# Block inverse of the gated delta rule: its 32- and 64-wide levels as tile products of the new blocks alone, the other triangle by transposing

## The chip, the cores and the metric

The kernel runs on one core of a Trainium2 chip, as one program with one launch. The metric is the time of an execution on the device in microseconds (us). In the profile PE is the tensor engine's matrix products, PEld its weight loads, DVE the vector engine, ACT the scalar engine, POOL the general engine, SP the engine that issues most transfers.

## The reference, cut to what matters

The program is two transformer blocks on 256 tokens of width 1024. The change lies in the first block's second layer, a gated delta rule with eight heads, 128 channels a head and, in the reference, chunks of 64 tokens:

```python
decay = jnp.exp(jnp.where(causal, g[..., :, None] - g[..., None, :], -jnp.inf))
a = jnp.einsum('bhncd,bhnmd->bhncm', k_beta, k) * decay
m = jnp.where(strict, a, 0.0) + jnp.eye(CHUNK, dtype=jnp.float32)
rhs = jnp.concatenate([v * beta[..., None], k_beta * jnp.exp(g)[..., None]], axis=-1)
sol = lax.linalg.triangular_solve(m, rhs, left_side=True, lower=True, unit_diagonal=True)
...
def step(state, xs):
    u_c, w_c, qk_c, qd_c, kd_c, gl_c = xs
    v_new = u_c - jnp.einsum('bhcd,bhde->bhce', w_c, state)
    o_c = (jnp.einsum('bhcd,bhde->bhce', qd_c, state)
           + jnp.einsum('bhcm,bhme->bhce', qk_c, v_new))
    state = state * gl_c[..., None, None] + jnp.einsum('bhcd,bhce->bhde', kd_c, v_new)
    return state, o_c
```

So in each head and chunk a unit lower triangular system is solved. The kernel takes chunks of 128 tokens, two halves of the 256, and inverts the 128x128 triangular matrix of each head and half.

## The kernel before

The program runs in phases (a pooling layer, an MLP, the delta rule, an MLP, an attention and gating mixer, a gated MLP, a last layer). Engines run their own queues in order; a scheduler fills these queues from the order in which the program is written, moves work that is ready ahead, and is held by `after("pe")` (L274), which lets an instruction be issued only behind the last matrix product recorded in `ends["pe"]`. No order is written by hand beyond the list `steps` in `gdn` (L508).

The matrices of four heads go together: a *chain* is a half h and a group g of four heads, four chains in all. Each has a tile `Ls` (128 tokens, 4 heads, 128 tokens; the negated strictly triangular part, tile name L), `Ts` (the inverse so far, lower triangle, tile name bc, one tile for both halves of a group) and `Rs` (its transposed, upper triangle, tile name Rm). `solve_base` (L630) inverts the 16x16 diagonal blocks on the vector engine and makes `Rs` by a transposition.

Then the inverse is built up in three levels (`LEVELS`, L25: 16, 32, 64): two neighbouring blocks of that width are joined to one of twice the width. `level_up` (L690) forms Y = L'R over the whole 128x128 matrix, four heads, and multiplies it with a mask `ups[li]` that keeps only the corner blocks that are new at this level (rows of the even block, columns of the odd one). `level_down` (L695) forms R·Y and adds it to R; unless the level is the last, it also forms the transposed product and adds it to T. `products` (L658) issues four products, one a head, into one PSUM bank; each is an fp32 product of 128x128 by 128x128. Banks come from three pools: psa (four buffers), psm and psc (two each).

`steps` (L757) runs first `sides` (transposed keys and values, key-query products) for the four chains, then the levels in a skewed order: at step t the down of the item two back, then the up of item t; the items are level 0 of the four chains, level 1 of the four, level 2 of the four. So a chain's up and down are two steps apart, and a chain comes back with its next level after four. Behind them stand `solution` (L702, R times the right-hand side), the new state, the output, and the output projection, whose weights (in_gdn_w_out) are cast on ACT (L141) and subtracted on DVE (L142) while the levels run.

Of the kernel before, what the change touches and what calls it, by code (L numbers as in the profile page):

```python
# [13 lines left out]
ALU = mybir.AluOpType  # L14
AX = mybir.AxisListType
P = 128
# [7 lines left out]
BASE = 16  # L24
LEVELS = (16, 32, 64)  # L25


def shape_constants():

    i = np.arange(P)  # L30
    a, b = i[:, None], i[None, :]
    f = np.float32
    ident = (a == b).astype(f)
    cum = np.concatenate([(a <= b).astype(f), np.ones((P, P), f)], 1)
    causal = np.concatenate([np.zeros((P, P), f), np.where(b <= a, f(0), f(NEG))], 1)
    block = (a // BASE == b // BASE).astype(f)
    ups = [((a // (2 * s) == b // (2 * s)) & ((a // s) % 2 == 0) & ((b // s) % 2 == 1)).astype(f) for s in LEVELS]
    sel = np.zeros((P, 16), f)
    for r in range(0, P, 32):
        sel[r : r + 16] = -np.eye(16)  # L40
    tri = np.concatenate([ident, cum, causal, block] + ups, 1)
    pos = np.arange(T)
    near, far = [], []
    for w in WINDOWS:
        m = ((pos[:, None] <= pos[None, :]) & (pos[None, :] - pos[:, None] < w)) / np.minimum(pos + 1, w)[None, :]
        m = (m - np.eye(T)).astype(f)
        near.append(m[:P, :EDGE])
        far.append(m[P:, P:])
    return np.ascontiguousarray(tri), np.ascontiguousarray(np.concatenate(near + far, 1)), sel
# [3 lines left out]
def tile_two_blocks(ctx: ExitStack, tc: tile.TileContext, I, tri_d, band_d, sel_d, out):  # L53
    nc = tc.nc
    pe, act, dve, pool, sp = nc.tensor, nc.scalar, nc.vector, nc.gpsimd, nc.sync
# [18 lines left out]
    def work(shape, tag, bufs, dt=F32):  # L74

        return ph[0].tile(shape, dt, tag=tag, bufs=bufs, name=f"{tag}_{next(ids)}")
# [12 lines left out]
    def bank(k):  # L89
        return banks[k].tile([P, 512], F32, tag=k, name=f"ps{k}_{next(ids)}")  # L90

    def quads(k):
        return bank(k).rearrange("p (a t) -> p a t", t=P)
# [6 lines left out]
    ident = cp.tile([P, P], F32, name="ident")  # L100
    tri = cp.tile([P, tri_d.shape[1] - P], F32, name="tri")
    cumf = tri[:, 0 : 2 * P]
    cumu, ones = cumf[:, :P], cumf[:, P:]
    causal = tri[:, 2 * P : 4 * P]
    block = tri[:, 4 * P : 5 * P]
    ups = [tri[:, (5 + i) * P : (6 + i) * P] for i in range(len(LEVELS))]
    mhalf = cp.tile([P, 16], F32, name="mhalf")
    pool.memset(mhalf, -0.5)

# [161 lines left out]
    ends = {}  # L271
# [230 lines left out]
    def bc4(m):  # L502
        return m.unsqueeze(1).to_broadcast([P, 4, P])
# [4 lines left out]
    def gdn(xs, X, then):  # L508
# [37 lines left out]
        for h in range(2):  # L546
            ps = bank("c")
            pe.matmul(ps[:, 0:8], cumu, gg[:, h, :], start=True, stop=True)
            pe.matmul(ps[:, 8:16], ones, gg[:, h, :], start=True, stop=True)
            a, b, c = (cp.tile([P, 8], F32, name=f"{n}{h}") for n in ("gc", "eg", "ed"))  # L550
# [38 lines left out]
        Ls, Ts, Rs = {}, {}, {}  # L589
# [68 lines left out]
        def products(bk, lhs, rhs):  # L658

            ps = quads(bk)  # L660
            for a in range(4):
                ends["pe"] = pe.matmul(ps[:, a, :], lhs[:, a, :], rhs[:, a, :], start=True, stop=True).ins
            return ps
# [23 lines left out]

        rhs, kd, state, Ym, xv, ob = {}, {}, {}, {}, {}, {}

        def level_up(c, li):  # L690
            yp = products("a", Ls[c], Rs[c])
            Ym[c] = work([P, 4, P], "Ym", 2)
            dve.tensor_tensor(Ym[c], yp, bc4(ups[li]), ALU.mult)

        def level_down(c, li):  # L695
            rp = products("m", Ts[c], Ym[c])
            if li < len(LEVELS) - 1:
                tp = products("c", Ym[c], Ts[c])
                dve.tensor_tensor(Ts[c], tp, Ts[c], ALU.add)
            dve.tensor_tensor(Rs[c], rp, Rs[c], ALU.add)  # L700

        def solution(h, g):  # L702
            xp = products("a", Rs[h, g], rhs[h, g])
# [53 lines left out]
        steps = [(sides, c) for c in chains]  # L757
        up_down = [(c, li) for li in range(len(LEVELS)) for c in chains]
        for t in range(len(up_down) + 2):
            if t > 1:  # L760
                steps.append((level_down, up_down[t - 2]))
            if t < len(up_down):
                steps.append((level_up, up_down[t]))
        pair = lambda f, *a: [(f, (*a, g)) for g in range(2)]
        steps += pair(solution, 0)
        for g in range(2):
# [331 lines left out]
    with phase("gdn"):  # L1098
        xs, X, emb = gdn(xs, X, lambda: layer_normed(lgs[1, 0], lbs[1, 0]))
# [38 lines left out]
```

## Time and profile before

| what | us |
|---|---|
| median of 3 runs (range) | 1129.73 (1128.65 to 1130.77) |
| the profiled execution | 1129.11 |
| its span in the profile | 1127.4 |
| first up product of level 0 | at 359.36 |
| first product of `solution` | at 388.93 |

A profile's group line reads: source line, engine, operation, tiles written and read, shape, count; then the time in which at least one of them ran, the mean duration of one in ns, and the idle time of the engine ahead of them with what ended it. A matrix product in fp32 leaves two records in the trace, a transposition one. Their durations overlap, since products are pipelined, so the price of one is the distance between starts. "L662" is the product line of the helper `products`, which serves many places; tile names tell them apart. Engine idle time matters only on the engine that sets the length of a stretch.

### The profile page before, as it was taken

To read this page: it belongs to the slowest core of one execution; us is meant where nothing else is said; L and a number is where in the kernel's file an instruction comes from. 1 tells how busy PE (TensorE), PEld (TensorE's weight loads), DVE (VectorE), ACT (ScalarE), POOL (GpSimd) and SP (SyncE) were. 2 spreads that over 40 slices of the span, in tenths; PEclk is the share of its full clock that TensorE was granted. 3 is DMA by queue.
4 is the path that set the end of the run, shared out by engine and by line. 5 is a ranking of instruction groups with operands and counts; after the bars stand their busy time and mean duration, and the time that the engine had idled before them with its cause. 6 is when DMAs were issued, how large, how long until landed. Compare 5 with 4: busy or idle time off the path is not lost. (4 is left out here: it accounts for less than half of the span.)

```text
span 1127.4 us, 17109 instructions
## 1 busy us (share of the span) xinstructions
PE 1098.7 (97%) x6546; PEld 964.2 (86%) x6546; DVE 798.4 (71%) x1265; ACT 603.4 (54%) x982; POOL 79.6 (7%) x78
## 2 busy tenths in 40 slices
PE   7999999999999999999999999999999999999997
PEld 5688888899999988788888788898888799999986
DVE  5865555688898668755557775587786867677784
ACT  1754544556656155554546456566664655555663
POOL 1001111110201010011101200000000000000000
PEclk9999999999999999999999999999999999999999
DMA  9665656545446035865666656565435745666650
GB/s 338 226 214 186 195 181 200 182 139 171 115 121 185 20 112 187 262 195 184 198 185 212 206 166 186 141 198 170 132 113 168 216 149 185 188 190 180 188 203 38
DMA packets 145250, 197.92 MB, mean 176 GB/s; under 512 B 11136, under 2 KB 117648, under 8 KB 145168
## 3 DMA queue, kind: packets, MB, share of 16 engines
q1 hardware_dynamic: 145167, 196.83, 56.6%
q8 instruction: 51, 0.84, 0.3%
q14 instruction: 32, 0.25, 0.1%
HBM read 195.49 MB, written 1.31 MB: 175 GB/s over the span
## 5 line engine op out<-in xcount | busy, mean ns | idle before, releaser
L142 DVE TENSOR_TENSOR lo<-raw,hi 128x1024 fp32r<-128x1024 f32 (+4 forms) x322 | 383.1, 1199 | 176.7 <-ACT hi L141 172.4
L141 ACT CAST hi<-raw 128x1024 fp32r<-128x1024 f32 (+4 forms) x322 | 330.8, 1031 | 175.4 <-PE psm L243 54.8
L243 PE MATMUL psm<-X,hi 128*128 128x512 f32 x864 | 308.3, 400 | 2.6 <-DVE sum L246 2.6
L244 PE MATMUL psm<-X,lo 128*128 128x256 f32 x864 | 242.2, 280 | 0.0
L243 PEld LDWEIGHTS psm<-X,hi 128*128 128x128 f32 x864 | 162.2, 188 | 44.7 <-DVE sum L246 4.7
L244 PEld LDWEIGHTS psm<-X,lo 128*128 128x128 f32 x864 | 163.1, 189 | 1.1
L153 PE MATMUL psm<-X,lo 128*128 128x256 f32 x448 | 127.1, 284 | 0.5 <-DVE lo L142 0.5
L152 PE MATMUL psm<-X,hi 128*128 128x256 f32 x448 | 126.9, 283 | 0.0
L151 PE MATMUL psm<-X,hi 128*128 128x256 f32 x448 | 126.9, 284 | 0.0
L151 PE MATMUL psa<-hi,hh 128*128 128x512 f32 x296 | 115.6, 391 | 0.0
L152 PE MATMUL psa<-lo,hh 128*128 128x512 f32 x296 | 115.5, 390 | 0.0
L153 PE MATMUL psa<-hi,hl 128*128 128x512 f32 x296 | 115.2, 389 | 0.0
L153 PEld LDWEIGHTS psm<-X,lo 128*128 128x128 f32 x448 | 85.9, 192 | 0.7 <-DVE lo L142 0.7
L151 PEld LDWEIGHTS psm<-X,hi 128*128 128x128 f32 x448 | 85.8, 192 | 0.6 <-ACT X L193 0.2
L152 PEld LDWEIGHTS psm<-X,hi 128*128 128x128 f32 x448 | 86.0, 192 | 0.3
L245 ACT COPY sum<-psm 128x256 f32<-128x256 f32 x120 | 44.1, 367 | 63.0 <-PE psm L244 62.8
L152 PE MATMUL psa<-lo,X 128*128 128x512 f32 (+5 forms) x212 | 76.0, 359 | 1.7 <-DVE lo L142 1.7
L151 PE MATMUL psa<-hi,X 128*128 128x512 f32 (+5 forms) x212 | 76.2, 360 | 0.5 <-ACT hi L141 0.5
L246 DVE TENSOR_TENSOR sum<-psm,sum 128x256 f32<-128x256 f32 x120 | 50.4, 420 | 37.1 <-ACT sum L245 37.1
L153 PE MATMUL psa<-hi,X 128*128 128x512 f32 (+5 forms) x212 | 75.9, 358 | 0.0
L451 POOL TENSOR_TENSOR hl<-sum,hh 128x512 fp32r<-128x512 f32 x32 | 43.4, 1355 | 330.8 <-ACT hh L450 164.8
L153 PEld LDWEIGHTS psa<-hi,hl 128*128 128x128 f32 x296 | 55.6, 188 | 11.9
(340 smaller groups left out, 1723.1 us busy)
## 6 DMA issues: line engine op xcount, KB each, us to landing
raw<-in_mlp_w_dram SPq DMA_DIRECT2D x128, 512.0 KB, 4.1
raw<-in_w_in_dram SPq DMA_DIRECT2D x48, 512.0 KB, 4.7
raw<-in_w_up_dram SPq DMA_DIRECT2D x44, 512.0 KB, 4.1
raw<-in_gdn_w_in_dram SPq DMA_DIRECT2D x24, 512.0 KB, 4.5
raw<-in_w_down_dram SPq DMA_DIRECT2D x22, 512.0 KB, 4.5
raw<-in_ple_gate_w_dram SPq DMA_DIRECT2D x16, 512.0 KB, 6.0
raw<-in_gdn_w_out_dram SPq DMA_DIRECT2D x8, 512.0 KB, 5.0
raw<-in_w_branch_a_dram SPq DMA_DIRECT2D x8, 512.0 KB, 4.9
```

The source lines that it names most:

```text
L141: act.copy(hi, raw)
L142: dve.tensor_tensor(lo, raw, hi.bitcast(F32), ALU.subtract)
L151: pe.matmul(o, lh, rh, start=start, stop=False)
L152: pe.matmul(o, lh, rl, start=False, stop=False)
L153: ends["pe"] = pe.matmul(o, ll, rh, start=False, stop=stop).ins
L243: pe.matmul(ps, wh, X.parts(k), start=k == 0, stop=False)
L244: ends["pe"] = pe.matmul(ps[:, 1, :], wl, X.hi(k), start=False, stop=k == 7).ins
L245: act.copy(y[:, f, :], ps[:, 0, :])
L246: dve.tensor_tensor(y[:, f, :], ps[:, 1, :], y[:, f, :], ALU.add)
L451: pool.tensor_tensor(hl, r, hh.bitcast(F32), ALU.subtract)
```

## The change

Level 0 keeps its full-width products with the mask. At levels 1 and 2 `level_up` and `level_down` now compute the corner blocks alone: for each head and each corner one product of 32x32 (two corners a head, so eight products a group) or 64x64 (one corner a head, four products). The results are copied out without mask or addition, since a corner is empty before: Y by DVE, R by ACT. The transposed product and its addition are gone at every level; `level_turn` transposes R instead and copies the result to T on ACT, four steps behind the up: whole 128x128 matrices after level 0, the upper left 64x64 after level 1, none after level 2. Only the mask of level 0 is left, so the constant tensor `tri` is 256 columns narrower.

```diff
-    ups = [tri[:, (5 + i) * P : (6 + i) * P] for i in range(len(LEVELS))]
+    ups = tri[:, 5 * P : 6 * P]
...
+        def corners(li):
+
+            n = LEVELS[li]
+            return [(slice(i, i + n), slice(i + n, i + 2 * n)) for i in range(0, P, 2 * n)]
+
         def level_up(c, li):
-            yp = products("a", Ls[c], Rs[c])
             Ym[c] = work([P, 4, P], "Ym", 2)
-            dve.tensor_tensor(Ym[c], yp, bc4(ups[li]), ALU.mult)
+            if li == 0:
+                dve.tensor_tensor(Ym[c], products("a", Ls[c], Rs[c]), bc4(ups), ALU.mult)
+                return
+            ps = quads("a")
+            for a in range(4):
+                for ev, od in corners(li):
+                    ends["pe"] = pe.matmul(ps[ev, a, od], Ls[c][od, a, ev], Rs[c][od, a, od], start=True, stop=True).ins
+            for ev, od in corners(li):
+                dve.tensor_copy(Ym[c][ev, :, od], ps[ev, :, od])
 
         def level_down(c, li):
-            rp = products("m", Ts[c], Ym[c])
-            if li < len(LEVELS) - 1:
-                tp = products("c", Ym[c], Ts[c])
-                dve.tensor_tensor(Ts[c], tp, Ts[c], ALU.add)
-            dve.tensor_tensor(Rs[c], rp, Rs[c], ALU.add)
+            if li == 0:
+                dve.tensor_tensor(Rs[c], products("m", Ts[c], Ym[c]), Rs[c], ALU.add)
+                return
+            ps = quads("m")
+            for a in range(4):
+                for ev, od in corners(li):
+                    ends["pe"] = pe.matmul(ps[ev, a, od], Ts[c][ev, a, ev], Ym[c][ev, a, od], start=True, stop=True).ins
+            for ev, od in corners(li):
+                act.copy(Rs[c][ev, :, od], ps[ev, :, od])
+
+        def level_turn(c, li):
+
+            ps, n = quads("c"), P if li == 0 else P // 2
+            for a in range(4):
+                ends["pe"] = pe.transpose(ps[:n, a, :n], Rs[c][:n, a, :n], ident[:n, :n]).ins
+            act.copy(Ts[c][:n, :, :n], ps[:n, :, :n])
...
             if t < len(up_down):
                 steps.append((level_up, up_down[t]))
+            if 4 <= t < len(up_down):
+                steps.append((level_turn, up_down[t - 4]))
```

In the changed file the up products of levels 1 and 2 stand on line L704, their copies on L706, the down products on L715, their copies on L717, the transpositions on L723, their copies on L724; the masks are L699 and the additions to R L710.

The first place is PE from the first chain's up of level 1 on. Before, full groups stood there in a row (psa is an up, psm a down for R, psc a down for T; behind the arrow the moving tile and the weights):

```order
L662 MATMUL psa_3581<-Rm_2698,L_2401 128x128 x4
L662 MATMUL psm_3588<-Ym_3567,bc_2617 128x128 x4
L662 MATMUL psc_3593<-bc_2617,Ym_3567 128x128 x4
L662 MATMUL psa_3600<-Rm_2718,L_2607 128x128 x4
L662 MATMUL psm_3607<-Ym_3586,bc_2411 128x128 x4
```

Now the same place holds, up to the end of the 32-wide items:

```order
L704 MATMUL psa_3564<-Rm_2698,L_2401 32x32 x8
L723 MATMUL psc_3575<-ident,Rm_2698 128x128 x4
L662 MATMUL psm_3581<-Ym_3550,bc_2617 128x128 x4
L704 MATMUL psa_3588<-Rm_2718,L_2607 32x32 x8
L723 MATMUL psc_3599<-ident,Rm_2718 128x128 x4
L715 MATMUL psm_3605<-Ym_3563,bc_2411 32x32 x8
L704 MATMUL psa_3617<-Rm_2708,L_2433 32x32 x8
L723 MATMUL psc_3628<-ident,Rm_2708 128x128 x4
L715 MATMUL psm_3634<-Ym_3587,bc_2617 32x32 x8
L704 MATMUL psa_3646<-Rm_2728,L_2639 32x32 x8
L723 MATMUL psc_3657<-ident,Rm_2728 128x128 x4
L715 MATMUL psm_3663<-Ym_3616,bc_2411 32x32 x8
```

The third group of each step is a transposition in place of the product for T, and tiles of 32 and of 128 take turns. Level 2 follows directly on PE:

```order
L704 MATMUL psa_3675<-Rm_2698,L_2401 64x64 x4
L723 MATMUL psc_3681<-ident,Rm_2698 64x64 x4
L715 MATMUL psm_3687<-Ym_3645,bc_2617 32x32 x8
L704 MATMUL psa_3699<-Rm_2718,L_2607 64x64 x4
L723 MATMUL psc_3705<-ident,Rm_2718 64x64 x4
L715 MATMUL psm_3711<-Ym_3674,bc_2411 64x64 x4
L704 MATMUL psa_3718<-Rm_2708,L_2433 64x64 x4
L723 MATMUL psc_3724<-ident,Rm_2708 64x64 x4
```

From there to the solutions all groups are 64 wide but the one of 32. The second place is DVE around the weight subtraction L142 that lies among the levels. Before:

```order
L693 TENSOR_TENSOR Ym_3548<-psa_3543,tri 128x512
L142 TENSOR_TENSOR qkv_3965<-raw_3963,qkv_3964 128x1024
L699 TENSOR_TENSOR bc_2617<-psc_3555,bc_2617 128x512
L700 TENSOR_TENSOR Rm_2718<-psm_3550,Rm_2718 128x512
L693 TENSOR_TENSOR Ym_3567<-psa_3562,tri 128x512
```

Now (Ym_3550 is the mask of the fourth chain at level 0, which psm_3581 above reads):

```order
L699 TENSOR_TENSOR Ym_3537<-psa_3538,tri 128x512
L710 TENSOR_TENSOR Rm_2718<-psm_3544,Rm_2718 128x512
L142 TENSOR_TENSOR qkv_4005<-raw_4003,qkv_4004 128x1024
L699 TENSOR_TENSOR Ym_3550<-psa_3551,tri 128x512
L710 TENSOR_TENSOR Rm_2708<-psm_3557,Rm_2708 128x512
L706 COPY Ym_3563<-psa_3564 32x4x32 x2
```

The subtraction stands directly ahead of the fourth mask; the additions to T are gone, and from level 1 on each step has two small copies. The third place is ACT, which had nothing between the weight cast and the solutions' copies:

```order
L141 CAST qkv_3964<-raw_3963 128x1024
L705 COPY Ym_3726<-psa_3721 128x512
L705 COPY Ym_3733<-psa_3728 128x512
L710 COPY L_3740<-psm_3735 128x512
L732 ACTIVATE sq_3747,co_2385<-psa_3742 128x128 x3
```

Now the copies to T and R stand between them:

```order
L141 CAST qkv_4004<-raw_4003 128x1024
L724 COPY bc_2411<-psc_3575 128x512
L724 COPY bc_2617<-psc_3599 128x512
L717 COPY Rm_2698<-psm_3605 32x4x32 x2
L724 COPY bc_2411<-psc_3628 128x512
L717 COPY Rm_2718<-psm_3634 32x4x32 x2
L724 COPY bc_2617<-psc_3657 128x512
```

They come behind the cast, which waits for a transfer of weights.

More of the change, by code (lines that the diff above doesn't have):

```diff
@@ L36, in shape_constants @@
     block = (a // BASE == b // BASE).astype(f)
-    ups = [((a // (2 * s) == b // (2 * s)) & ((a // s) % 2 == 0) & ((b // s) % 2 == 1)).astype(f) for s in LEVELS]
+    ups = ((a // (2 * BASE) == b // (2 * BASE)) & ((a // BASE) % 2 == 0) & ((b // BASE) % 2 == 1)).astype(f)
     sel = np.zeros((P, 16), f)
@@ L40, in shape_constants @@
         sel[r : r + 16] = -np.eye(16)
-    tri = np.concatenate([ident, cum, causal, block] + ups, 1)
+    tri = np.concatenate([ident, cum, causal, block, ups], 1)
     pos = np.arange(T)
```

## The prediction

> **What bounds the kernel now.** I read the page's busy shares first, then the granted clock and busy time of the block inverse and of what follows it, then that stretch's groups and its timeline.
>
> ```profile
> PE 1098.7 (97%) x6546; PEld 964.2 (86%) x6546; DVE 798.4 (71%) x1265; ACT 603.4 (54%) x982; POOL 79.6 (7%) x78
> ```
>
> TensorE (PE) is busy 97% of the span, so a microsecond taken from PE inside the inverse should reach the end, if the inverse itself is bound by PE. The windows answer that; behind the busy times stand the granted clock, the DMA share and GB/s.
>
> ```profile
> 359.36:361.90 2.54, 1.95 (x18) 1.79 (x17) 2.54 (x6) 1.47 (x8) 0.00 (x0) 1.00 0.00 0
> 361.90:388.93 27.03, 27.03 (x240) 26.95 (x241) 21.27 (x31) 1.05 (x1) 0.00 (x0) 1.00 0.13 40
> 388.93:414.93 26.00, 25.16 (x172) 22.63 (x170) 14.04 (x39) 17.79 (x56) 4.03 (x4) 1.00 0.23 81
> ```
>
> The three levels run from 359.36 to 388.93, 29.57 us. After one wait at the start PE never stops (27.03 of 27.03); VectorE (DVE) has 5.8 us spare, ScalarE (ACT) works 1.05 us, the DMA queues rest, the clock is full. PE alone sets the length. In its groups (busy, mean ns, idle before):
>
> ```profile
> L662 PE MATMUL psm<-Ym,bc 128*128 128x128 f32 x96 | 12.7, 277 | 0.6 <-DVE Ym L693 0.6
> L662 PE MATMUL psa<-Rm,L 128*128 128x128 f32 x96 | 12.5, 275 | 0.0
> L662 PE MATMUL psc<-bc,Ym 128*128 128x128 f32 x64 | 8.5, 275 | 0.0
> L693 DVE TENSOR_TENSOR Ym<-psa,tri 128x512 f32<-128x512 f32 x12 | 8.2, 689 | 1.8 <-PE psa L662 1.8
> L700 DVE TENSOR_TENSOR Rm<-psm,Rm 128x512 f32<-128x512 f32 x12 | 8.3, 690 | 2.7 <-PE psm L662 2.7
> L699 DVE TENSOR_TENSOR bc<-psc,bc 128x512 f32<-128x512 f32 x8 | 5.5, 690 | 1.2 <-PE psc L662 1.2
> ```
>
> An fp32 product of four heads leaves eight records; 96+96+64 records are 32 such groups. The busy times are unions with overlap, so the price is taken from starts:
>
> ```profile
> 361.07 1.28 DVE L693 TENSOR_TENSOR Ym<-psa,tri 128x512 f32<-128x512 f32 x2
> 361.90 1.13 PE L662 MATMUL psm<-Ym,bc 128*128 128x128 f32 x8 [0.59 <-DVE Ym L693]
> ...
> 377.16 1.06 PE L662 MATMUL psa<-Rm,L 128*128 128x128 f32 x8
> 378.06 1.06 PE L662 MATMUL psm<-Ym,bc 128*128 128x128 f32 x8
> 378.25 0.69 DVE L693 TENSOR_TENSOR Ym<-psa,tri 128x512 f32<-128x512 f32 x1 [0.20 <-PE psa L662]
> ```
>
> Group to group is 0.894 us (377.16 to 378.06), 0.112 a record. DVE starts 0.03 behind the last record's end (377.16 + 1.06 = 378.22). Two groups from 359.36 fill PE to 361.15; the third starts at 361.90, since VectorE comes late to the first mask (361.07; two in 1.28, so the first ends near 361.75): a wait of 0.65 beyond the usual step. 32 x 0.894 = 28.6, this wait and 0.3 at the end make the 29.57.
>
> **The change, step by step.** Level 0 (16 wide) keeps four up and four down groups: 8 x 0.894 = 7.15, and the wait of 0.65. Its four transposed products go; four transpositions come, of four records each:
>
> ```profile
> 356.05 0.60 PE L668 MATMUL psc<-ident,qkv 128*128 128x128 f32 x4
> 356.49 0.83 PE L662 MATMUL psa<-qkv,qkv 128*128 128x128 f32 x6
> ```
>
> 0.44 a group, 1.75 in all. Levels 1 and 2 had 20 full groups, 17.9 us. Now level 1 has eight groups of eight 32x32 products (16 records if fp32 still leaves two) and four of 64x64 transpositions; level 2 has eight groups of four 64x64 products. No row shows such a tile. Bounds come from how a record scales with the moving width:
>
> ```profile
> L372 PE MATMUL psa<-pw,pl 128*128 128x256 f32 x32 | 7.1, 379 | 0.0
> 264.05 0.37 PE L549 MATMUL psc<-gg,tri 128*128 128x8 f32 x2
> 264.27 0.37 PE L548 MATMUL psc<-gg,tri 128*128 128x8 f32 x2
> 791.31 1.14 PE L926 MATMUL psa<-bc,m 128*64 128x128 f32 x12
> ```
>
> At 256 columns a record is 7.1/32 = 0.222, twice the 0.112 at 128: no fixed part shows. So 64 wide is 0.056 and 32 wide 0.028, half of that (0.014) if a group's two corners, which lie in different rows and columns of the array, run at once. The other end is the product with eight moving columns and full weights: two records in 0.22, still 0.11. The nearest row is L926, weights 64 wide in two halves of the array: (1.14 - 0.28)/11 = 0.078 a record, 1.4 times the 0.055 of two perfect halves, at twice to four times our widths. I take 0.035 for a 32-wide record (0.028 and a quarter more), corners one after the other, and 0.056 for a 64-wide one. Level 1: 8 x 16 x 0.035 = 4.5; level 2: 8 x 8 x 0.056 = 3.6; the small transpositions 16 x 0.055 = 0.9.
>
> Changing the tile has a price in the trace, where 128-row products meet a 44-row transposition and where they meet L926:
>
> ```profile
> 911.39 0.28 PE L152 MATMUL psm<-X,hi 128*128 128x256 f32 x1
> 911.51 0.28 PE L153 MATMUL psm<-X,lo 128*128 128x256 f32 x1
> 911.72 0.25 PE L123 MATMUL psc<-ident,rows 44*128 44x44 f32 x1
> 911.90 0.39 PE L151 MATMUL psm<-X,hi 128*128 128x256 f32 x1
> 791.10 0.28 PE L244 MATMUL psm<-X,lo 128*128 128x256 f32 x1
> ```
>
> The usual step behind such a record is 0.12 (911.39 to 911.51). Here it is 0.21 into the small tile, and into L926 likewise 0.21 (791.10 to 791.31): 0.09 per change of tile. The new order has 13 changes (128 to 32 and back for each turn, then 32 to 64): 1.2 us. The Trainium skill ("TensorEngine Tiling (Array Packing)", Key Properties) says that changing the tiling mode drains TensorE; the trace agrees, with 0.09 us. Without a drain the sum would be 1.2 shorter. The same page (Gotcha 1: PSUM Pressure) says that different row tiles cannot access one PSUM bank at once; both corners of a group write one bank, and no run here shows such a pair. By it the corners go one after the other, 0.56 a group; without it 0.28, 2.2 us less in all.
>
> Waits. New hops run over ACT, and the copies are small:
>
> ```profile
> 909.10 0.27 ACT L124 COPY taps<-psc 128x128 f32<-128x128 f32 x1 [0.48 <-PE psc L123]
> 264.45 0.17 DVE L551 COPY gc<-psc 128x8 f32<-128x8 f32 x1 [0.24 <-PE psc L549]
> 390.02 0.59 ACT L705 COPY Ym<-psa 128x512 f32<-128x512 f32 x1 [24.21 <-PE psa L662]
> 364.77 1.05 ACT L141 CAST qkv<-raw 128x1024 fp32r<-128x1024 f32 x1 [3.64 <-DMA raw<-in_gdn_w_out_dram]
> 365.85 1.23 DVE L142 TENSOR_TENSOR qkv<-raw,qkv 128x1024 fp32r<-128x1024 f32 x1 [0.30 <-ACT qkv L141]
> ```
>
> A 32x4x32 copy is 128 elements a row: 0.27 on ACT; on DVE, between 0.17 at eight elements and 0.69 at 512, about 0.3. In a level-1 turn of the order PE has 0.56 down, 0.56 up, 0.44 transposition and two changes, 1.74 us; ACT has 2 x 0.27 + 0.59 = 1.13, DVE 0.6, and each result has a turn or more before its reader. ACT and DVE hide there; if a 32-row copy cost as much as a full one (0.59), ACT's 1.77 would just match PE. Two waits do show. The weight cast at 364.77 stands ahead of ACT's first turn copy; it ends at 365.82 and by the sum PE ends that turn's transpositions after 367, so this costs nothing (were the transfer late, every turn copy would queue behind it). On DVE its subtraction (365.85 to 367.08) stands ahead of the mask of the fourth chain: that mask ends near 367.7, and the fourth down group, due near 367.5 by the sum, waits 0.3. At the end the last down group waits 0.2 for its copy, since no other group is left to cover it.
>
> The sum: 7.15 + 0.65 + 1.75 + 4.5 + 3.6 + 0.9 + 1.2 + 0.5 + 0.1 = 20.35 us against 29.57: 9.2 less. DVE's 13 us fewer count nothing, being hidden already. The mask tensor's transfer shrinks by a quarter, which is hidden:
>
> ```profile
> L1095 SPq DMA_DIRECT2D tri<-in_tri_dram x1: 327/327/327, 14.7 to 14.7; - x1
> ...
> DMA to landing us min/median/max: 7.3/7.3/7.3
> ```
>
> It lands near 22 us, and the first reader shown above (L549 at 264.05) comes 240 us later. No other transfer changes its place in SP's queue, and POOL's order stays. Behind the inverse PE is busy 25.16 of 26.00 with DMA at 0.23, and weights for the next stage are fetched when their buffers come free, which moves with PE: I let the gain through. The profiled execution took 1129.11 us (span 1127.4); 9.2 less is 1119.9. The median shown, 1129.73, is 0.62 higher, so the forecast for a median is **1120.5**.
>
> **Rivals.** *Corners overlap*: a 32-wide group costs 0.28, ACT's 1.13 still fits into the 1.18 of a turn, and 11.4 us go: 1118.3. For it: in L926 the two halves do run together. Against: those share their rows. *Small records have a floor of some 0.06, or waits of 0.3 in ten turns*: all but the small records is 10.85 us (7.15 + 0.65 + 1.75 + 1.2 + 0.1), and 208 of them (128 + 64 + 16) at 0.062 make 12.9, together 23.75, 5.8 less: 1123.9. L926's 0.078 speaks for it, L372 against. The Trainium skill ("TensorE: Matmul & The Clock Gate", "Wait — 56ns, not 53.3ns?") gives 62 ns of sequencer time per MATMUL with hardware decode off and a 25 ns floor otherwise; the rows are too wide to decide. *A flat record price, slower than before*: a record costs 0.11 whatever its width, as L549's does. 208 x 0.111 + 10.85 = 33.9, 4.4 more: 1134.1. It turns slower from 0.090 a record on, (29.57 - 10.85)/208. L926's 0.078 is below that and L549 has full-width weights, so I hold it unlikely. *The gain is lost behind the inverse*: PE would have to wait 9 us there for weights; it is idle 0.84 of those 26.00 now. No change, 1129.
>
> **How the numbers follow.** Forecast (8 to 10.5 us less) 0.52; overlap 0.15; floor or waits (3 to 8 less) 0.20; flat price 0.08; lost 0.05. The range goes from the overlap's far end, 1117.5, to 1125.5, which is a record of 0.07; what lies beyond is the flat price, the lost gain and the dear end of the floor. 0.2% is 2.3 us, about what a measurement can tell here. Faster 0.87, no change 0.05, slower 0.08.
>
> **What would show it.** The solutions (two groups reading Rm with rhs) should start near 380 instead of 388.93; L704 and L715 starts give the record price directly; the step between a 32-wide group and a full transposition shows the change of tile; PE's idle time ahead of L662 and L715 shows the waits. The prediction is wrong if a 32-wide group takes over 0.9 us, if PE waits for ACT copies in every turn, or if the stretch from 389 to 460 grows by what the inverse loses.

## The result and the profile after

| | before | after |
|---|---|---|
| median of 4 runs (range), us | 1129.19 (1127.41 to 1130.77) | 1119.45 (1118.92 to 1121.0) |
| the profiled execution, us | 1129.11 | 1119.24 |
| its span, us | 1127.4 | 1117.5 |
| first up product to first `solution` product, us | 29.57 | 19.03 |
| from there to the end of the span, us | 738.46 | 737.86 |

The ratio of the medians is 0.9916, with a 95% interval of 0.9898 to 0.9935: the change saves 9.7 us. Forecast were 9.2, and 1120.5 us. The three levels are now 10.54 us shorter, and what follows them is as long as it was to within 0.6 us; this execution came to the levels 1.3 us later than that of before (360.64 against 359.36), which hides a part of it in the span.

The busy times on the page of the changed kernel:

```profile
PE 1088.5 (97%) x6578; PEld 952.1 (85%) x6578; DVE 785.9 (70%) x1253; ACT 609.4 (55%) x1002; POOL 79.3 (7%) x78
```

PE has 10.2 us less work than the 1098.7 of before, DVE 12.5 less. Its windows, columns as in the prediction; the second starts with the solutions:

```profile
360.64:379.67 19.03, 18.18 (x290) 16.04 (x288) 11.94 (x25) 9.10 (x29) 0.00 (x0) 1.00 0.16 57
379.67:405.67 26.00, 25.27 (x171) 22.73 (x169) 13.26 (x38) 18.12 (x57) 4.03 (x4) 1.00 0.25 81
```

PE is busy 18.18 of 19.03 us in the levels: it still sets their length. ACT went from 1.05 to 9.10 us there, and the last column of PE's groups (idle time ahead, and what ended it) names no wait for it:

```profile
L704 PE MATMUL psa<-Rm,L 32*32 32x32 f32 (+1 forms) x96 | 4.5, 204 | 0.0
L662 PE MATMUL psm<-Ym,bc 128*128 128x128 f32 x32 | 4.4, 281 | 0.9 <-DVE Ym L699 0.9
L715 PE MATMUL psm<-Ym,bc 32*32 32x32 f32 (+1 forms) x96 | 4.4, 204 | 0.0
L723 PE MATMUL psc<-ident,Rm 128*128 128x128 f32 (+1 forms) x32 | 4.3, 255 | 0.0
```

The only waits in that column are two for a mask, 0.9 us in all. The timeline of the changed kernel shows what a group takes. The rows are PE's, but for four copies at the end.

```profile
366.83 1.06 PE L662 MATMUL psm<-Ym,bc 128*128 128x128 f32 x8
367.82 0.44 PE L704 MATMUL psa<-Rm,L 32*32 32x32 f32 x16
368.19 0.66 PE L723 MATMUL psc<-ident,Rm 128*128 128x128 f32 x4
369.11 1.16 PE L662 MATMUL psm<-Ym,bc 128*128 128x128 f32 x8 [0.26 <-DVE Ym L699]
370.20 0.44 PE L704 MATMUL psa<-Rm,L 32*32 32x32 f32 x16
370.57 0.66 PE L723 MATMUL psc<-ident,Rm 128*128 128x128 f32 x4
371.15 0.34 PE L715 MATMUL psm<-Ym,bc 32*32 32x32 f32 x10
371.31 0.22 PE L704 MATMUL psa<-Rm,L 32*32 32x32 f32 x2
371.33 0.22 PE L715 MATMUL psm<-Ym,bc 32*32 32x32 f32 x3
371.37 0.19 PE L704 MATMUL psa<-Rm,L 32*32 32x32 f32 x1
...
371.69 0.66 PE L723 MATMUL psc<-ident,Rm 128*128 128x128 f32 x4
372.27 0.34 PE L715 MATMUL psm<-Ym,bc 32*32 32x32 f32 x10
...
373.39 0.44 PE L715 MATMUL psm<-Ym,bc 32*32 32x32 f32 x16
373.76 0.68 PE L704 MATMUL psa<-Rm,L 64*64 64x64 f32 x8
374.36 0.41 PE L723 MATMUL psc<-ident,Rm 64*64 64x64 f32 x4
374.70 0.44 PE L715 MATMUL psm<-Ym,bc 32*32 32x32 f32 x16
...
369.57 0.59 DVE L706 COPY Ym<-psa 32x128 f32<-32x128 f32 x2
371.74 0.52 ACT L717 COPY Rm<-psm 32x128 f32<-32x128 f32 x2
376.18 0.36 ACT L724 COPY bc<-psc 64x256 f32<-64x256 f32 x1 [0.47 <-PE psc L723]
378.65 0.36 ACT L724 COPY bc<-psc 64x256 f32<-64x256 f32 x1 [0.32 <-PE psc L723]
```

Three readings. A 32-wide group of 16 records takes 0.44 us from its first start to its last end, and a record of that width ends 0.19 after its start (371.37), so its starts cover 0.25 us: 0.0167 a record, not 0.035. A level-1 turn (down, up, transposition) goes from 371.15 to 372.27, 1.12 us, where 1.74 was forecast. And at 371.31 the first product of the next group starts while the group ahead of it has not started all of its own (371.33): groups that work in other rows of the array overlap at their borders. The last four rows are small copies: 0.3 on DVE, 0.26 on ACT, 0.36 for a 64-wide one. Each but the one in the last row is done before its reader comes. That one, ACT's last copy to T, ends at 379.01; the group that reads it starts at 379.07, 0.12 us behind the record ahead of it where 0.058 is usual, a wait of some 0.07.

### The profile page after: what moved, and what is told of

Same layout as the page of the kernel before. It is cut to its first block, busy times and chain, and to the rows that moved or that the text cites. A ratio compares the mean times of both kernels' runs of the same rounds, so it can differ in the third digit from the quotient of the medians.

```text
span 1117.5 us, 17195 instructions
## 1 busy us (share of the span) xinstructions
PE 1088.5 (97%) x6578; PEld 952.1 (85%) x6578; DVE 785.9 (70%) x1253; ACT 609.4 (55%) x1002; POOL 79.3 (7%) x78
## 5 line engine op out<-in xcount | busy, mean ns | idle before, releaser
L142 DVE TENSOR_TENSOR lo<-raw,hi 128x1024 fp32r<-128x1024 f32 (+4 forms) x322 | 383.0, 1198 | 176.6 <-ACT hi L141 172.3
L151 PEld LDWEIGHTS psa<-hi,hh 128*128 128x128 f32 x296 | 55.6, 188 | 11.9
```

The costliest lines, as they stand in the source:

```text
L142: dve.tensor_tensor(lo, raw, hi.bitcast(F32), ALU.subtract)
L151: pe.matmul(o, lh, rh, start=start, stop=False)
```

## The experiments

Between kernels the length of the levels is compared, from the first up product to the first `solution` product in the profiled execution; a median stands beside it where there is one. Eleven runs follow: of eight further kernels, one of them twice, and of the changed kernel twice more.

**The transposition alone.** Levels 1 and 2 keep full products and masks; only the product for T and its addition give way to `level_turn`, with the whole 128x128 matrix after levels 0 and 1.

```diff
-            rp = products("m", Ts[c], Ym[c])
-            if li < len(LEVELS) - 1:
-                tp = products("c", Ym[c], Ts[c])
-                dve.tensor_tensor(Ts[c], tp, Ts[c], ALU.add)
-            dve.tensor_tensor(Rs[c], rp, Rs[c], ALU.add)
+            dve.tensor_tensor(Rs[c], products("m", Ts[c], Ym[c]), Rs[c], ALU.add)
...
+                ends["pe"] = pe.transpose(ps[:, a, :], Rs[c][:, a, :], ident).ins
+            act.copy(Ts[c], ps)
```

> One part alone: the kernel before with full 128x128 products and masks at all three levels, but the product for T replaced by transposing R at levels 0 and 1. Theory A (PE sets the length of the inverse; a full fp32 group costs 0.894 us, a full transposition group 0.44): eight groups of 0.894 go, eight of 0.44 come, so the stretch from the first up to the first solution falls from 29.57 to about 25.9 us and the time by about 3.6 us. No tile changes, so no steps over 0.12 us between groups. Rival B (the gain of the whole change comes mostly from the transposing and from relieving DVE, the small tiles only break even): 7 to 10 us less here.

The windows of this kernel, the levels alone:

```profile
358.43:384.40 25.97, 25.37 (x226) 25.11 (x225) 18.48 (x28) 7.21 (x18) 0.00 (x0) 1.00 0.13 41
```

25.97 us, 3.6 less than before. That is eight times the step of a full product less that of a transposition, 8 x (0.894 - 0.44) = 3.6: at one tile size the records' prices simply add up. Its median is 1125.26 us, ratio 0.9968 (0.9951 to 0.9984), 3.6 us below the 1128.82 of the kernel before beside it: what PE saves in the levels reaches the end.

**The tiles alone.** Corner products as in the change; T is still made by products, full at level 0 and a 32-wide corner at level 1.

```diff
-                dve.tensor_tensor(Rs[c], products("m", Ts[c], Ym[c]), Rs[c], ALU.add)
+                rp = products("m", Ts[c], Ym[c])
+                dve.tensor_tensor(Ts[c], products("c", Ym[c], Ts[c]), Ts[c], ALU.add)
+                dve.tensor_tensor(Rs[c], rp, Rs[c], ALU.add)
...
+                ends["pe"] = pe.matmul(ps[od, a, ev], Ym[c][ev, a, od], Ts[c][ev, a, ev], start=True, stop=True).ins
+            dve.tensor_copy(Ts[c][od, :, ev], ps[od, :, ev])
```

> The other part alone: 32- and 64-wide tile products as in the changed kernel, but T is not transposed: level 0 forms it by the full product as before, level 1 by a 32x32 product of its one needed corner (four products a chain), copied by DVE. Theory A: against the changed kernel four full groups (3.6 us) come at level 0; four full transposition groups with their tile changes go (0.67 each, 2.7), four 64-wide ones with theirs go (0.43 each, 1.7), four 32-wide groups of 0.25 come (1.0, or nothing where they overlap). Stretch 18.5 to 20.5 us against 19.03 in the changed kernel; new waits for DVE and ACT copies are possible, since a turn would hold under 0.8 us of PE work. Rival B (small tiles only break even): 25 to 29 us.

The levels took 21.58 us, but not all at one clock. In its windows the granted clock is the third number from the end:

```profile
358.49:374.00 15.51, 14.59 (x240) 13.81 (x239) 13.40 (x28) 3.67 (x15) 0.00 (x0) 1.00 0.20 69
374.00:376.00 2.00, 2.00 (x41) 1.82 (x40) 0.92 (x3) 0.90 (x4) 0.00 (x0) 0.52 0.05 12
378.00:380.07 2.07, 1.96 (x21) 1.68 (x19) 0.42 (x1) 0.73 (x2) 0.00 (x0) 0.50 0.00 0
```

About 6 us of the stretch, from 374 to its end at 380.07, ran at half the clock. Were those 6 us wholly PE's, they would be 3 at full clock, and the levels some 18.6; for the changed kernel the same correction (below) comes out 0.6 too low, so 18.6 to 19.3 is my estimate, about the length of the whole change. By this estimate the tiles alone bring nearly all of the gain, and the transposition, worth 3.6 by itself, adds next to nothing to them; no profile of this kernel at full clock was taken. The median, 1121.62 us (0.9927; 0.9898 to 0.9956), holds executions caught in this way and does not contradict it: the quickest of the five is 1117.37.

**The corners one after the other.** The two loops over heads and corners change places, so that four products of one corner stand ahead of four of the other.

```diff
-            for a in range(4):
-                for ev, od in corners(li):
+            for ev, od in corners(li):
+                for a in range(4):
```

> The changed kernel with the two loops of the 32-wide products swapped, so that the four heads of one corner come first and then those of the other. Theory A (two corners in different rows and columns of the array run at once, 0.0315 us a pair; within a corner a record takes 0.0315): a 32-wide group takes 0.4 to 0.5 us instead of 0.25 and the stretch grows by 1.2 to 2 us (eight groups). Rival C (the pair step of 0.0315 is the rate at which PE issues two records and their loads, whatever the place): a group stays at 0.25 and the stretch at 19.0.

From its timeline, ahead of a stretch at half clock:

```profile
364.16 0.59 PE L704 MATMUL psa<-Rm,L 32*32 32x32 f32 x16
364.68 0.66 PE L723 MATMUL psc<-ident,Rm 128*128 128x128 f32 x4
```

The same 16 records take 0.59 where they took 0.44, so 0.40 from first to last start instead of 0.25. Only the order in the queue differs. In the changed kernel a record of each corner starts every 0.0315 us, the two 0.006 apart; within one corner, as here, a single record takes these 0.0315. So in the changed kernel the two corners do run at once, as the rival *Corners overlap* had it, though they write one PSUM bank; the Trainium skill ("TensorEngine Tiling (Array Packing)", Gotcha 1: PSUM Pressure) would have kept them apart, and the rows go against it here. The levels as a whole took 22.62 us with the clock halved from 373 on, so their length decides nothing.

**The 64-wide transposition as a product by the identity.** In the changed kernel's timeline L723 at 374.36 follows L704 at 373.76 by 0.60 us, where eight records at 0.058 would be 0.46. Of the difference, 0.05 is the late second record of the up (it stands behind 32-wide tiles), and 0.09 lies directly ahead of L723. If the transposition is a change of tile for PE though its tile has the same size, a product in its place should close that gap, at twice the records.

```diff
-                ends["pe"] = pe.transpose(ps[:n, a, :n], Rs[c][:n, a, :n], ident[:n, :n]).ins
+                if li == 0:
+                    ends["pe"] = pe.transpose(ps[:n, a, :n], Rs[c][:n, a, :n], ident[:n, :n]).ins
+                else:
+                    ends["pe"] = pe.matmul(ps[:n, a, :n], Rs[c][:n, a, :n], ident[:n, :n], start=True, stop=True).ins
```

> The changed kernel with the 64-wide transposition of level 1 done as an ordinary fp32 product with the identity (eight records of 0.058 a group instead of four of 0.056). Theory A1 (the idle 0.09 on either side of a 64-wide transposition comes from the change between transposition and product in tiles under 128): these gaps go, the group may even start while the up before it still runs, and the time from the up's last record to the next down's first stays at 0.45 or falls; stretch 18.3 to 19.1 us. Rival A2 (the gaps come from the change of rows between an up, rows 64 to 127, and what follows): the gaps stay and each of the four groups costs 0.23 more; stretch near 20.0.

Its timeline (L726 is the new product):

```profile
372.25 0.50 PE L704 MATMUL psa<-Rm,L 64*64 64x64 f32 x5
372.54 0.27 PE L726 MATMUL psc<-ident,Rm 64*64 64x64 f32 x1
372.59 0.22 PE L704 MATMUL psa<-Rm,L 64*64 64x64 f32 x1
...
374.02 0.45 PE L726 MATMUL psc<-ident,Rm 64*64 64x64 f32 x5
374.31 0.45 PE L715 MATMUL psm<-Ym,bc 64*64 64x64 f32 x5
```

The gap is gone: L726 starts at 372.54 among the records of L704, and L715 follows at the usual step (five records from 374.02 to 374.31, 0.058 each). The levels took 18.56 us with twice the records in these four groups. So the transposition acts as a change of tile. The Trainium skill ("TensorEngine Tiling (Array Packing)", Restrictions) says that column tiling disables the transpose mode for fp32 input; that would fit these rows, which show the gap but not its reason.

The same kernel once more:

> The changed kernel with the 64-wide transpositions written as products by the identity, once more, timed in rounds beside the kernel before. Theory A1 (the 64-wide transposition is a change of tile for TensorE, the same product is not): the levels take 18.5 to 18.7 us against 19.03, and the median lies 0.5 us below that of the changed kernel, within what the measurement can tell. Rival A2: what the one look showed (1117.17) was the clock alone, and the median is that of the changed kernel.

The levels took 18.66 us, as theory A1 had it; median 1118.57 (1116.86 to 1120.09), ratio 0.9913 (0.9899 to 0.9926). Against the changed kernel the levels lose 0.4 us; the medians (the changed kernel's was 1119.64 in the same series) are too close to tell.

**Pairs.** Two items at a time: both downs, both ups, both transpositions, which leaves fewer changes of tile.

```diff
+        duos = [up_down[i : i + 2] for i in range(0, len(up_down), 2)]
+        for t in range(len(duos) + 1):
+            if t > 0:
+                steps += [(level_down, x) for x in duos[t - 1]]
+            if t < len(duos):
+                steps += [(level_up, x) for x in duos[t]]
+            if 2 <= t < len(duos):
+                steps += [(level_turn, x) for x in duos[t - 2]]
```

> The changed kernel with its steps written in pairs of chains (two downs, two ups, two turns), so that tiles of one width stand together: the same products and copies, half the changes of tile. Theory A (each change costs 0.09 us of drain and 0.015 to 0.10 at the next group's second record): some 12 of 26 changes go (64-wide transpositions count as changes), stretch 17.3 to 18.3 us instead of 19.03. Rival (waits for DVE and ACT copies take over, since a pair's results are wanted sooner): 19 us or more.

And the same with the 64-wide transposition as a product:

> The pairs of the run before with the 64-wide transposition as a product with the identity (18.56 us in its run alone). Theory A: both savings add but for what they share, since pairs leave only half of those changes: stretch 17.0 to 18.0 us; time about 2 us under the changed kernel's if the clock holds. Under theory H the level-1 stretch has fewer full-width products close to the small ones in any window, so a halved clock should come in more executions than in the changed kernel and take the 2 us back in these.

The first took 22.56 us, part of it at half clock (from 376 on). The second ran its levels at full clock and yet took 20.96 us. PE's waits there (engine line, from whom: us in total, times, longest):

```profile
PE psm L662 <- DVE Ym L699: 1.9, 2, 1.3
PE psm L715 <- ACT bc L727: 0.5, 2, 0.2
```

The wait for the fourth chain's mask grew from 0.26 to 1.3 us: on DVE that mask still stands behind the weight subtraction, and PE, whose next work is a down of the same pair, now has nothing else to do. And copies by ACT are waited for in two turns, in the changed kernel only at the end. PE is busy 18.36 of 20.96 us. The medians agree: 1120.14, ratio 0.9919 (0.9899 to 0.9939), no gain over the changed kernel. The fewer changes of tile cost more waiting than they save. Nor did the clock halve in more executions than in the changed kernel, against theory H: of six, one at a mean clock of 0.994 is unclear, and the others ran at 0.996 or more.

**Only the transpositions in pairs.** Downs and ups keep their skewed order, with the 64-wide product.

```diff
-            if 4 <= t < len(up_down):
-                steps.append((level_turn, up_down[t - 4]))
+            if 4 <= t < len(up_down) and t % 2 == 0:
+                steps += [(level_turn, x) for x in up_down[t - 4 : t - 2]]
```

> As the kernel with the 64-wide product, with the transpositions issued two by two in every second step, each still four items or three behind its up. On TensorE the 32-wide groups then stand between 128-wide ones four times fewer. Theory T (each change of tile costs 0.09 us ahead and 0.10 us at the second record behind it): 4 x 0.19 = 0.8 us less than the 18.56 of the kernel with the turns one by one, the levels in 17.6 to 18.0 us. Rival W (the waits take over, as they did where whole pairs of items were moved): the second transposition of a pair waits for its R or the next product for the copies, and the levels take 18.5 us or more. Either way under 1 us, which times alone will not tell; the trace has to.

The windows of this kernel, and a level-1 stretch of its timeline:

```profile
358.26:375.97 17.71, 16.80 (x306) 15.67 (x304) 11.94 (x25) 9.12 (x29) 0.00 (x0) 1.00 0.19 62
```

```profile
368.60 1.09 PE L724 MATMUL psc<-ident,Rm 128*128 128x128 f32 x8
369.62 0.34 PE L715 MATMUL psm<-Ym,bc 32*32 32x32 f32 x10
369.78 0.22 PE L704 MATMUL psa<-Rm,L 32*32 32x32 f32 x2
...
370.31 0.50 PE L704 MATMUL psa<-Rm,L 64*64 64x64 f32 x5
```

Three 32-wide groups now go from 369.62 to 370.31, 0.69 us with the change behind them. The levels took 17.71 us, 0.95 less than with the turns one by one (18.66), with waits of 0.9 against 1.0. Four changes of tile are gone, expected at 0.8; how much of the rest is the overlap of neighbouring groups was not measured apart. The median is 1116.21 (1115.35 to 1117.53), ratio 0.9889 (0.9877 to 0.9902), the lowest of all; its interval still overlaps that of the changed kernel run beside it (1119.64; 0.9894 to 0.9943). So the trace shows it 1.3 us ahead in the levels, and the times alone do not settle it.

**Full products among the tiles.** The kernel with the tiles alone, and ahead of each 32- or 64-wide up one full group more, whose result nobody reads.

```diff
+            products("a", Ls[c], Rs[c])
             ps = quads("a")
```

> The kernel of e2_tiles_only, which ran at a mean clock of 0.992 to 0.996, with one full-width product group a chain added ahead of each up of levels 1 and 2, whose result nobody reads (eight groups, 7.15 us of PE). Theory H: full-width work now stands in every window of 3.4 us, the clock stays whole, mean 0.996 to 0.998, and the stretch is 26 to 28 us (18.8 for e2 without the halved clock, 7.15 for the groups, some 16 changes of tile, less the waits of e2 that they cover). Rival (it is the small tiles themselves, however mixed, or chance): mean clock 0.992 to 0.995 again in most executions and a stretch of 30 us or more.

```profile
358.30:385.65 27.35, 26.44 (x387) 24.73 (x385) 15.76 (x33) 5.67 (x21) 0.00 (x0) 1.00 0.12 40
```

The window above holds its levels: 27.35 us at full clock. Eight groups at 0.894 are 7.15; on the 18.6 to 19.3 estimated for the tiles alone that leaves 0.9 to 1.6 us, for up to sixteen more changes of tile. The median is 1128.27, ratio 0.9982 (0.9968 to 0.9997). Its mean clock was 0.995 or more in each of ten executions, close to theory H's 0.996 to 0.998, where three of five with the tiles alone lay at 0.992 to 0.994. So in these runs the long fall of the clock does not come where full products stand among the tiles; that a window of 3.4 us decides it, no run shows.

**The changed kernel again,** twice:

> The changed kernel once more, unchanged, to have its time and the clock of its executions on the same chip as the next ones. Theory H (the granted clock halves for 10.24 us where a window of some 3.4 us holds little but small tiles, and where such windows fall differs from execution to execution): most executions at a mean clock of 0.996 to 0.998 as the first four (0.997, 0.995, 0.997, 0.996), a few at 0.995 or below and 2 us longer. Rival (the clock of the changed kernel is as before's in every execution): mean clocks as before's, 0.996 to 0.999, and no longer executions.

> The changed kernel itself, beside the two others on the same chip. Unless the clock is halved in it, the levels take 19.0 us; where the clock is halved for 10.24 us among them or behind them, as in its last profile, 21 us and a median some 5 us higher.

The first series gave a median of 1116.82 (1115.11 to 1124.49; ratio 0.9906, 0.9877 to 0.9935), the second 1119.64 (1113.7 to 1124.48; 0.9918, 0.9894 to 0.9943). In each, two of six executions took 1122.5 us or more with a mean clock of 0.990 to 0.992; the other eight ran at 0.995 or more, in 1120.5 or less. Windows of one of these four, from the second series (1122.52 us):

```profile
370.00:372.00 2.00, 2.00 (x72) 1.75 (x72) 1.12 (x5) 1.77 (x6) 0.00 (x0) 1.00 0.10 37
372.00:374.00 2.00, 2.00 (x48) 1.59 (x47) 0.73 (x3) 1.50 (x5) 0.00 (x0) 1.00 0.00 0
374.00:376.00 2.00, 2.00 (x29) 1.72 (x30) 0.42 (x1) 1.26 (x5) 0.00 (x0) 0.87 0.00 0
376.00:378.00 2.00, 2.00 (x21) 1.71 (x21) 0.42 (x1) 0.73 (x2) 0.00 (x0) 0.50 0.04 12
...
384.00:386.00 2.00, 2.00 (x13) 2.00 (x12) 0.00 (x0) 0.65 (x2) 0.00 (x0) 0.57 0.00 0
386.00:388.00 2.00, 2.00 (x21) 2.00 (x20) 0.00 (x0) 1.63 (x8) 0.00 (x0) 1.00 0.00 0
```

The clock falls to a half among the 64-wide tiles (0.87 and 0.57 are mixed windows; the missing parts add up to 10.2 us at half clock) and comes back behind the solutions; the step of a 64-wide record grows from 0.058 to 0.107 us with it. The levels took 20.95 us here, 5.0 of them at half clock (375.50 to 380.45): halving those gives 18.5, against the 19.03 measured at full clock, so the correction overshoots by 0.6, in part because the step does not quite double. Ten microseconds at half clock are at most 5.1 us of lost work; the four lie 7.0 us above the mean of the other eight, so this is the larger part of what parts them, and theory H, with 2 us, had put it too low. The profile of the first series (1123.90 us) has a second, shorter stretch at half clock ahead of the levels, from 346.1 to 349.5.

## Why the prediction was right, by its own steps

The time, the range and the sign held, and so did the mechanism in the main: the levels are bound by PE, so what PE saves there reaches the end. The solutions start at 379.67 (forecast: near 380), and the stretch behind grew by nothing (25.27 of 26.00 busy, against 25.16 before), so the rival by which the gain is lost behind the inverse is out. The flat record price (0.11), the floor (0.062) and waits in ten turns are out too: a 32-wide record costs 0.0167 and a 64-wide one 0.058, and PE waits for a mask twice. What did not hold is the step that runs the two corners one after the other; there the rival was right, at a chance of 0.15.

The 19.03 us as steps from one group's start to the next in PE's timeline, by kind, so each with the change of tile behind it, beside the sum's terms:

| | forecast | measured |
|---|---|---|
| level 0 and its first wait | 7.15 + 0.65 | 8.27 |
| eight 32-wide groups | 4.5 | 2.55 |
| four full transpositions | 1.75 | 2.67, with the mask's wait |
| eight 64-wide groups | 3.6 | 4.18, with the last wait |
| four 64-wide transpositions | 0.9 | 1.36 |
| changes of tile | 1.2 | in the rows above |
| new waits | 0.5 + 0.1 | in the rows above |
| sum | 20.35 | 19.03 |

So the total came out 1.3 us too high by two wrong terms of opposite sign. That it came so near is in part luck: with the 32-wide term alone set right, at 2.0, the sum would have been 17.9, 1.2 too low. The saving in the medians, 9.7 us in the first series, was 12.5 and 9.85 in the two later ones.

- **The 32-wide term was mis-sized**: "0.035 for a 32-wide record, corners one after the other", 0.56 a group. It is 0.25, near the rival's 0.28, because the two corners run at once; the experiment with the loops exchanged shows that. The quarter more leaned on a misread row: the 0.078 of L926 is no surcharge on a small tile. In its trace the records of one half stand 0.109 apart, much like the 0.112 of a full record of the same moving width, and the second half's first record starts at 791.581, 0.006 behind the third of the first half. So 0.078 is a mean over records alone and records side by side, and the trace of before had two parts of the array at work at once wherever their records met.
- **The term for changes of tile was mis-sized the other way**: 13 at 0.09, 1.2 us. The records at their own prices come to 7.15 + 2.0 + 1.75 + 3.7 + 0.9 = 15.5, and the waits, from start to start, to 0.76 + 0.42 + 0.07 = 1.25, as much as was set aside; what is left of the 19.03, some 2.3 us, is my estimate for the changes. There are 20, since each 64-wide transposition is a change into and out of itself. And 0.09 is only the gap ahead: the second record behind a change is late as well. The full transposition at 368.19 shows it, 0.66 long behind 32-wide tiles where the one at 356.05 of before took 0.60.
- The 64-wide record (0.058 against 0.056), the small copies (0.26 to 0.36) and the hidden ACT and DVE were as forecast. The fourth mask's wait, forecast at 0.3, is 0.26 of idle time and 0.42 from start to start (368.19 to 369.11 is 0.92, of which the group and its late second record are 0.50). For ACT PE waited once, 0.07 at the last group instead of 0.2.
- Two small terms are off: the first wait in the trace of before is 361.90 - 361.15 = 0.75, not 0.65 (0.76 in the changed kernel), and the 0.1 at the end of the sum is explained nowhere and no run shows it; the two come to the right total.
- "11.4 less" for overlapping corners was too much for the same reason: that rival kept the cheap changes.

What the forecast did not see is that the two parts of the change do not add up: 3.6 us for the transposition and some 10.3 to 11 for the tiles (the estimate above), each alone, but 10.54 together. At level 0 the transpositions cost 2.67, with their changes of tile and a wait, where four full products cost 3.58; at level 1 they cost 1.36, where the tiles alone need only a 32-wide group that overlaps its neighbours.

Still open is why the clock halves. The Trainium skill ("TensorE: Matmul & The Clock Gate", Part 4: PE-mode transpose) says that a transposition does not count as busy PE in the same way; it cannot be the whole cause here, since the kernel with the tiles alone has no transposition in its levels and was caught. The kernels with the product in its place (one by one or two by two) had no such execution in ten, the changed kernel four in sixteen; that is too few to call them safe, and of the six with the product in pairs of items one is unclear.

## What to carry to other kernels

Where PE is the bound, shrink products to the blocks that are new, and put products of different rows and columns next to each other in the queue, so that they run at once. Count every change of tile, transpositions in fp32 among small tiles included, and sort the order so that equal tiles stand together, but only as far as the skew between producer and reader lasts: moving the transpositions alone gained 0.95 us, moving whole pairs of items brought 1.3 us waits. And do not add up two savings that remove the same work.

## What was not expected of the hardware

- **The clock can halve while PE is busy.** In the rows above PE was busy 2.00 of 2.00 us in the windows ahead of it. Stretches of 10.2 us came in five profiles of four kernels with dense small tiles, from 373 to 377 us on, with no idle gap over 0.3 us in the 7 us ahead, and in no profile of the kernel before, of the transposition alone, or of the one with full products among the tiles. The Trainium skill ("TensorE: Matmul & The Clock Gate", HAM oscillation — how this bites in real kernels) puts such a fall down to idle gaps of more than some 3.4 us; the longest wait in the changed kernel's levels is 0.6 us. Shorter stretches at half clock, of 3.4 us, occur in the kernel before too (at 265.9 us). In the profiles of before, of the changed kernel (its first and 1123.90 us), of the pairs with the product and of the full products among the tiles they begin 0.2 to 2.2 us behind an idle gap of PE of 1.2 to 2.6 us; that the gap brings them was not tested.
- **Products start out of program order** when they use other rows of the array: L704 at 371.31 ahead of the rest of L715 at 371.33.
- **Two corners of one group write one PSUM bank at once,** in partitions 0 to 31 and 64 to 95, at 0.0167 us a record.
